# A decoder layer on one core: heads' outputs copied by ScalarE and scaled in SBUF, router constants on ScalarE, other spacing of the compression, the modulation and the first routing

## The chip, the cores and the metric

The kernel runs as one program on one core of a Trainium2 chip. The metric is the time of one execution in microseconds on the device. Before is given as the median of three runs. Five engines work side by side, each through its own queue in the order of the program: TensorE (PE, matrix products; PEld is its loading of weights), VectorE (DVE), ScalarE (ACT), GpSimd (POOL) and SyncE (SP), which issues most transfers.

## What is computed

One decoder layer over 1024 tokens of width 1024, with random weights in float32. Two groups of channels read the same modulated and normalised input: an attention with three branches (compressed blocks, blocks chosen by score, a window), gated and added up, and a short gated convolution. Both go through a norm of 64 channels each and an output projection; a mixture of 64 experts follows.

```
sh1, sc1, g1, sh2, sc2, g2 = split(silu(c) @ w_ada + b_ada)        # six rows of 1024
h = rms_norm(x, norm1_w) * (1 + sc1) + sh1
q, kvs, gate_logits, b_gate, c_gate, u = split(h @ w_in)
k_c = rms_norm(compress(kv[:, :, 0], cmp_pos_k, cmp_k_w1, cmp_k_w2), k_norm_w[0])
v_c = compress(kv[:, :, 1], cmp_pos_v, cmp_v_w1, cmp_v_w2)   # silu(blocks @ w1) @ w2
o_attn = nsa_attention(q, gates, k_c, v_c, k_s, v_s, k_w, v_w, rel_bias)
         # three branches for each head: gates[..., i] * softmax(...) @ v, added up
y_conv = b_gate * short_conv(c_gate * u, conv_w)
mix = rms_norm over each 64 channels of concat(o_attn, y_conv)
x = x + g1 * (mix @ w_out)
h2 = rms_norm(x, norm2_w) * (1 + sc2) + sh2
x = x + g2 * hier_moe(h2, w_group, b_group, w_expert, b_expert, w1, w3, w2)
         # top 1 of 8 groups, top 2 of its 8 experts, 64 experts in all
```

## The kernel before

The kernel is one long program for the five engines. Its stages in the order of time are: a head (the first modulation row by matmuls, the norm and the transposes of the input), the projection, the attention, the rest of the output projection with the routing of the second half of the tokens, and the experts, whose weights are streamed through a ring of buffers while TensorE multiplies.

The projection is cut into jobs of 128 columns. `job(idx, ...)` runs 48 matmuls of 128 by 512 (lines 367 to 369: three for each of 8 k-steps and each of two halves of the tokens), into the PSUM tags "pp" and "st". A k-step ends with `yield`. What a job's result needs afterwards (the copy, the norm's root, transposes) is a generator in the list `posts`; `advance()` moves every such generator by one step, once in the middle of each half of a job and once at its end. `cmp_post(kvi)` is such a generator. It makes the compressed keys (kvi 0) or values (kvi 1): a shifted copy S of the projection, a bias added into Z (line 579), a product with the weights w1 in four pieces (line 590, into "acc"), the silu through e into hid (lines 596 to 599), a product with w2 (line 605 for keys, line 628 for values), and for the keys a norm of 64 columns, jk (line 613), and a transpose (line 616). `value_post` copies the values and transposes them (line 678).

Beside this stands a second generator, `mod_steps`: the five chunks of the relative bias table (`rel_steps`, lines 167 to 170: matmul, two copies by VectorE, a DMA to memory from POOL, the copy of the next chunk waiting for it), reads back and twelve exchange matmuls (line 193), and then the sums of the remaining two thirds of the modulation (`ada_sums`, lines 295 and 297: for each of 8 pieces of 128 rows of the weight, one VectorE instruction on 128 by 1024; 16 instructions for each of two rows of the modulation), the matmuls that add up the partitions (line 306), and `ada_done` with its transposes (line 272). Each load of weights for it is issued two pieces ahead. `first_job(steps)` moves `mod_steps` by one at some k-steps of a job, and what is left at the end is issued behind the gate job.

The PSUM tags "mx", "pp", "st" and "acc" have two buffers of 128 by 512 each; `ps(tag)` takes the next one, and an instruction that writes it waits until the last reader of its content two turns earlier is done. "mx" is used by the relative table, the compression, the modulation and the transposes of values; "acc" by the compression's product with w1, by the norms of the projections and by the outputs of heads.

The attention has 16 units (a head and a half of the queries). For each tile of scores, ScalarE takes two exponentials, P and PH, VectorE or POOL their difference PL, and TensorE multiplies PH and PL with the values into an accumulator of "acc" (lines 948 to 951). When a branch of a unit is complete, `take` scales it by gate over sum and adds it to oN. `merge` norms two heads, and transposes them (line 974). The second half of the attention also carries, as filler, the preparation of the output projection (`out_prepare`, with the router's constants, lines 1101 and 1108), its matmuls and `route(0)`, the routing of the first half of the tokens.

## Time and profile before

| | before |
|---|---|
| median of three runs | 1701.32 us |
| the runs, lowest and highest | 1697.93 and 1703.72 us |
| profiled execution | 1703.64 us |
| its span, first to last instruction | 1701.9 us |
| granted clock of TensorE, mean over the span | 0.967 |
| busy TensorE | 1537.3 us (90%) |
| busy VectorE | 711.5 us (42%) |
| busy ScalarE | 512.3 us (30%) |
| busy GpSimd | 356.8 us (21%) |

All durations and positions in the rows below are of this one profiled execution, in us from the start of its span. The shares are means over the whole span; the projection, the attention and the experts each have another mix. "Idle before, and what ended it" says which instruction released a waiting one.

### The profile page before, as it was taken

How to read it: one execution, taken by the hardware profiler on the slowest of the kernel's cores; microseconds unless marked ns; L12 is line 12 of the kernel's file. 1: busy time of each engine (PE TensorE's matmuls, PEld its weight loads, DVE VectorE, ACT ScalarE, POOL GpSimd, SP SyncE). 2: the span in 40 equal slices, each digit the busy share in tenths (PEclk: the TensorE clock that was granted, in tenths of full speed). 3: DMA queues.
4: the chain of work that ended last, by engine and by line, in shares of the span. 5: the costliest groups of instructions: out<-in, count | busy, mean ns of one | idle time of the engine just before them, and what ended most of it. 6: DMA issues, size and time to landing. Idle time of an engine off the chain costs nothing. (4 is left out here: it accounts for less than half of the span.)

```text
span 1701.9 us, 24631 instructions
## 1 busy us (share of the span) xinstructions
PE 1537.3 (90%) x9870; PEld 733.9 (43%) x9870; DVE 711.5 (42%) x1678; ACT 512.3 (30%) x992; POOL 356.8 (21%) x355
## 2 busy tenths in 40 slices
PE   5978988999889998969999998999999999899995
PEld 3434454555456664533443334333333333343431
DVE  3737675565798666581323123214113112131211
ACT  4654655565566664120201011101002011020100
POOL 4233453344475545010000000000000000000000
PEclk8899989999999999979999999999999999999998
DMA  9338541110241115669999999999999999999992
GB/s 352 102 114 261 155 110 44 36 39 17 64 158 46 40 33 188 246 257 399 427 425 427 427 424 428 426 426 427 427 427 427 427 426 426 426 426 429 426 428 112
DMA packets 84627, 480.82 MB, mean 283 GB/s; under 512 B 12551, under 2 KB 46552, under 8 KB 58652
## 3 DMA queue, kind: packets, MB, share of 16 engines
q1 hardware_dynamic: 76620, 461.16, 67.3%
q0 software_dynamic: 7744, 18.03, 2.9%
q8 instruction: 79, 1.29, 0.3%
q14 instruction: 40, 0.33, 0.1%
q10 hardware_dynamic: 144, 0.00, 0.0%
HBM read 473.20 MB, written 14.35 MB: 286 GB/s over the span
## 5 line engine op out<-in xcount | busy, mean ns | idle before, releaser
L1573 PE MATMUL ps<-wr,xs 128*64 128x512 f32 x2048 | 453.4, 597 | 1.8 <-DVE xs L1563 1.0
L1590 PE MATMUL ps<-wr,hT 128*64 128x512 f32 x1024 | 258.0, 608 | 44.3 <-DMA wr<-in_w_dram 42.8
L1573 PEld LDWEIGHTS ps<-wr,xs 128*64 128x64 f32 x2048 | 158.3, 138 | 289.7 <-issue 248.8
L1560 ACT ACTIVATE xs<-ps,sh2p,a2p 128x128 f32<-128x128 f32 x128 | 55.1, 455 | 565.7 <-DVE xs L1563 563.2
L1485 DVE TENSOR_TENSOR hid<-ps,hid 128x512 f32<-128x512 f32 x32 | 22.1, 691 | 417.3 <-PE ps L1573 417.3
L1627 POOL DMA_INDIRECT out_dram<-xg,toki x16 | 15.9, 997 | 793.9 <-DVE xg L1626 793.2
L1590 PEld LDWEIGHTS ps<-wr,hT 128*64 128x64 f32 x1024 | 79.2, 140 | 215.4 <-issue 148.5
L877 POOL TENSOR_TENSOR PL<-P,PH 128x384 f16<-128x384 f32 (+3 forms) x138 | 131.2, 956 | 172.9 <-ACT PH L873 85.7
L1593 DVE TENSOR_TENSOR y<-ps,lt 128x512 f32<-128x512 f32 x64 | 44.3, 692 | 250.3 <-PE ps L1590 250.3
L871 ACT ACTIVATE P<-st 128x512 f32<-128x512 f32 (+3 forms) x208 | 98.3, 472 | 110.8 <-PE st L929 88.4
L1622 PE MATMUL sum<-y,CT 128*128 128x512 f32 x256 | 115.3, 593 | 0.0
L367 PE MATMUL pp<-hi,wh 128*128 128x512 f16 x272 | 105.8, 391 | 3.5 <-ACT hi L435 3.5
L369 PE MATMUL pp<-hi,wl 128*128 128x512 f16 x272 | 106.1, 390 | 0.0
L368 PE MATMUL pp<-lo,wh 128*128 128x512 f16 x272 | 105.8, 389 | 0.0
L873 ACT ACTIVATE PH<-st 128x512 f16<-128x512 f32 (+3 forms) x208 | 98.0, 471 | 0.3
L1484 ACT ACTIVATE hid<-ps 128x512 f32<-128x512 f32 x32 | 19.1, 597 | 197.2 <-PE ps L1573 197.2
L1622 PEld LDWEIGHTS sum<-y,CT 128*128 128x128 f32 x256 | 46.1, 190 | 46.8 <-issue 46.0
L1563 DVE TENSOR_SCALAR xs<-ps,a2p,sh2p 128x128 f32<-128x128 f32 x128 | 49.5, 407 | 39.5 <-ACT xs L1560 27.7
L948 PE MATMUL acc<-VH,PH 128*128 128x65 f16 x528 | 59.6, 196 | 5.2 <-DVE ot L895 5.2
L1555 PE MATMUL ps<-Sm,xl 128*128 128x128 f16 x512 | 61.6, 220 | 2.5 <-DVE xl L1522 2.5
L1555 PE MATMUL ps<-Sm,xh 128*128 128x128 f16 x512 | 61.7, 220 | 1.6 <-ACT xh L1521 1.6
L919 PE MATMUL st<-QA,KA 128*128 128x512 f16 (+1 forms) x192 | 60.7, 316 | 1.7 <-ACT PH L873 1.5
(448 smaller groups left out, 2531.5 us busy)
## 6 DMA issues: line engine op xcount, KB each, us to landing
wr<-in_w_dram SPq DMA_DIRECT2D x189, 2048.0 KB
ada<-in_w_ada_dram SPq DMA_DIRECT2D x32, 512.0 KB
raw<-in_w_in_dram SPq DMA_DIRECT2D x22, 512.0 KB
ada<-in_w_ada_dram SPq DMA_DIRECT2D x8, 1024.0 KB
xt<-in_x_dram SPq DMA_DIRECT2D x8, 512.0 KB
x<-in_w_out_dram SPq DMA_DIRECT2D x8, 512.0 KB
wr<-in_w_dram SPq DMA_DIRECT2D x3, 1024.0 KB
w1t<-in_cmp_k_w_dram POOLq DMA_DIRECT2D x4, 512.0 KB, 4.8
```

The costliest lines, as they stand in the source:

```text
L367: PE.matmul(p, wh[:, k, :], hi[:, k, m], start=(k == 0), stop=False)
L368: PE.matmul(p, wh[:, k, :], lo[:, k, m], start=False, stop=False)
L369: job_pe[0] = PE.matmul(p, wl[:, k, :], hi[:, k, m], start=False, stop=(k == KT - 1)).ins
L871: ACT.activation(P[:, c], p[:, c], AF.Exp)
L873: ACT.activation(PH[:, c], p[:, c], AF.Exp)
L877: eng.tensor_sub(PL[:, c], P[:, c], PH[:, c])
L919: PE.matmul(p[:, c], KA[g][:, j, b, :], tq[:, c], start=True, stop=False)
L948: PE.matmul(o, PH[:, w_], vh, start=(first and q == q0), stop=False, skip_group_check=True)
L1555: pe(PE.matmul(q[:, k * 128:(k + 1) * 128], part[:, a, h, k, :], Sm[:, a, sl], start=(a == 0 and part is xh), stop=(a == 1 and part is xl)))
L1573: pe(PE.matmul(hp_[nm][64 * u:64 * u + 64, :], xs[:, k, 64 * u:64 * u + 64], wring[nm, 2 * P + u, k], start=(k == 0), stop=(k == KT - 1)))
L1590: pe(PE.matmul(q[64 * u:64 * u + 64, :], hT[:, f, 64 * u:64 * u + 64], wring["w2", 2 * P + u, f][:, n * 512:(n + 1) * 512], start=(f == 0) ...
L1622: pe(PE.matmul(sums[a][n], CT[:, a, :], y[:, n * 512:(n + 1) * 512], start=(p == 0), stop=(p == 3)))
```

## The change

A modulation step is taken after every second k-step instead of every third. In `cmp_post`, three steps lie between hid and its product and, for the keys, three between jk and its transpose, instead of two and one. The transposes of the values and of the modulation write "acc" instead of "mx". In `take`, ScalarE copies the 260 columns of the accumulator into SBUF first, VectorE works from the copy, and the tile ot is no more. The router's eight broadcast columns shb and the eight scalings of WR are done by ScalarE. The last merged pair's scaling is done by VectorE instead of POOL. `route(0)` has eight more steps.

```
@@ -267,7 +267,7 @@
         yield
         POOL.dma_start(modD[s].rearrange("h (c j) -> c h j", c=4), modrow[s][0:128:32, :].rearrange("c (h j) -> c h j", h=2))
         yield
-        pt = ps()
+        pt = ps("acc")
         for t in range(4):
             PE.transpose(pt[:, t * 128:(t + 1) * 128], modrow[s][:, t * 128:(t + 1) * 128], identf)
         V.tensor_copy(modc[:, s * 16:(s + 1) * 16].rearrange("p (h c t) -> p h c t", h=2, c=4),
@@ -597,8 +597,8 @@
                 V.tensor_scalar(e, e, 1.0, None, op0=ALU.add)
                 V.reciprocal(e, e)
                 V.tensor_mul(hid[:, t, :], ph[t], e)
-            yield
-            yield
+            for _ in range(3):
+                yield
             if kvi == 0:
                 pk = ps()
                 for t in range(2):
@@ -611,7 +611,8 @@
                 V.tensor_scalar(sk[:, 0:1], sk[:, 0:1], 1.0 / HD, EPS, op0=ALU.mult, op1=ALU.add)
                 POOL.tensor_tensor(sk[:, 1:2], sk[:, 0:1], mhalf[:, 0:1], op=ALU.pow)
                 V.scalar_tensor_tensor(jk, pks, sk[:, 1:2], knc, op0=ALU.mult, op1=ALU.mult)
-                yield
+                for _ in range(3):
+                    yield
                 pt = ps()
                 PE.transpose(pt[0:64, 0:128], jk, identf)
                 for g in range(2):
@@ -673,7 +674,7 @@
             ACT.activation(vt, p, AF.Copy, scale=1.0 / WS)
             yield
             yield
-            pt = ps()
+            pt = ps("acc")
             for j in range(4):
                 PE.transpose(pt[:, j * 128:(j + 1) * 128], vt[:, j * 128:(j + 1) * 128], identf)
             src = pt.rearrange("p (j g d) -> p j g d", j=4, g=2)
@@ -718,7 +719,7 @@
 
     def first_job(steps):
         for n_, _ in enumerate(steps):
-            if n_ % 3 == 2:
+            if n_ % 2:
                 with tc.issue_after(job_pe[0]):
                     next(mod_steps, None)
 
@@ -879,7 +880,8 @@
 
     def take(u, acc, n, gi):
         half, h = units[u]
-        av = acc[:, 0:260].rearrange("p (i c) -> p i c", i=4)
+        av = aw.tile([128, 4, 65], F32, name="av")
+        ACT.activation(av, acc[:, 0:260].rearrange("p (i c) -> p i c", i=4), AF.Copy)
         r = aw.tile([128, 4], F32, name="rr")
         V.scalar_tensor_tensor(r, av[:, :, 64], 1e-27, gates[:, half * 4:half * 4 + 4, h * 3 + gi],
                                op0=ALU.max, op1=ALU.mult)
@@ -891,9 +893,8 @@
         if n == 0:
             V.tensor_tensor(dst, av[:, :, 0:64], rb, op=ALU.mult)
         else:
-            ot = aw.tile([128, 4, 64], F32, name="ot")
-            V.tensor_tensor(ot, av[:, :, 0:64], rb, op=ALU.mult)
-            POOL.tensor_tensor(dst, dst, ot, op=ALU.add)
+            V.tensor_tensor(av[:, :, 0:64], av[:, :, 0:64], rb, op=ALU.mult)
+            POOL.tensor_tensor(dst, dst, av[:, :, 0:64], op=ALU.add)
 
     def slots_of(u):
         half = units[u][0]
@@ -965,7 +966,7 @@
         V.tensor_reduce(so, sq8, axis=AX.X, op=ALU.add)
         V.tensor_scalar(so, so, 1.0 / HD, EPS, op0=ALU.mult, op1=ALU.add)
         POOL.tensor_tensor(so, so, mhalf, op=ALU.pow)
-        POOL.tensor_tensor(sq8, o8, so[:, :, None].to_broadcast([128, 8, 64]), op=ALU.mult)
+        (V if pr == 7 else POOL).tensor_tensor(sq8, o8, so[:, :, None].to_broadcast([128, 8, 64]), op=ALU.mult)
         for _ in range(MERGE_LAG):
             yield
         with tc.issue_after(last_pe[0]):
@@ -1098,14 +1099,14 @@
         PE.matmul(pb[:, 0:72], ones[0:1, :], rb, start=True, stop=False)
         for k in range(KT):
             shb = rt.tile([128, 128], F32, name="shb")
-            V.tensor_copy(shb, SH2[:, k:k + 1].to_broadcast([128, 128]))
+            ACT.activation(shb, SH2[:, k:k + 1].to_broadcast([128, 128]), AF.Copy)
             PE.matmul(pb[:, 0:72], shb, WR[:, k, :], start=False, stop=(k == KT - 1))
         R["io"] = rt.tile([128, GCAP], BF, name="io", bufs=1)
         POOL.iota(R["io"], pattern=[[1, GCAP]], base=0, channel_multiplier=0, allow_small_or_imprecise_dtypes=True)
         R["rbias"] = rt.tile([128, 72], F32, name="rbias", bufs=1)
         V.tensor_copy(R["rbias"], pb[:, 0:72])
         for k in range(KT):
-            V.tensor_scalar(WR[:, k, :], WR[:, k, :], a2[:, k:k + 1], None, op0=ALU.mult)
+            ACT.activation(WR[:, k, :], WR[:, k, :], AF.Identity, scale=a2[:, k:k + 1])
         yield
 
     def out_part(t, ks):
@@ -1222,6 +1223,9 @@
         G = tile_(8, "G")
         V.tensor_tensor(G, row(io64[:, 0:8]), wide(gid, 8), op=ALU.is_equal)
         V.tensor_copy(GA[:, ts, 0:8], G)
+        if hb == 0:
+            yield
+            yield
         pg = ranks(ps(tag), 0, 8)
         payA = rt.tile([128, 4, 2], F32, name="payA", bufs=1)
         payA3 = rt.tile([128, 4, 3, 2], BF, name="payA3", bufs=1)
@@ -1237,6 +1241,9 @@
             oh = rt.tile([128, GCAP], BF, name="oh0", bufs=4)
             oh_ = V.tensor_scalar(oh, R["io"], t0[:, i, :], None, op0=ALU.is_equal)
             ohs.append(oh)
+        if hb == 0:
+            yield
+            yield
         table(tabA, payA3, 2, tabA if hb else crow[:, :, 6:8].to_broadcast([128, 2, 2]))
         if hb:
             V.tensor_copy(toki0, tabA[:, :, 0])
@@ -1263,6 +1270,9 @@
         V.tensor_tensor(es, eo[:, :, 0, :], eo[:, :, 1, :], op=ALU.add)
         V.tensor_tensor(GA[:, ts, 8:72].rearrange("p t (g e) -> p t g e", g=8), G[:, :, :, None].to_broadcast([128, 4, 8, 8]),
                         es[:, :, None, :].to_broadcast([128, 4, 8, 8]), op=ALU.mult)
+        if hb == 0:
+            yield
+            yield
         pe_ = ranks(ps(tag), 8, 64)
         if hb == 0:
             R["GS"] = rt.tile([128, 72], BF, name="GS", bufs=1)
@@ -1296,6 +1306,9 @@
 
         V.tensor_copy(payB3[:, :, 0, 0:2], sl1)
         V.tensor_sub(payB3[:, :, 1, 0:2], sl1, payB3[:, :, 0, 0:2])
+        if hb == 0:
+            yield
+            yield
         table(tab0, payB3, 4, tab0 if hb else crow[:, :, 1:5].to_broadcast([128, 2, 4]))
         V.tensor_scalar(ok, r01, float(CAP), None, op0=ALU.is_lt)
 
```

On TensorE in the projection, around line 616 (which is line 617 after the change), the transpose of the compressed keys; wh, wl, hi and lo are the operands of projection matmuls, nf those of the exchange matmuls. Before:

```order
L369 LDWEIGHTS wl
L369 MATMUL st<-hi,wl 128x512
L616 MATMUL mx<-identf,jk 64x128
L367 LDWEIGHTS wh
L367 MATMUL st<-hi,wh 128x512
L368 LDWEIGHTS wh
L368 MATMUL st<-lo,wh 128x512
L193 LDWEIGHTS exch
L193 MATMUL mx<-nf,exch 128x512
```

After:

```order
L369 LDWEIGHTS wl
L369 MATMUL pp<-hi,wl 128x512
L617 MATMUL mx<-identf,jk 64x128
L679 MATMUL acc<-identf,vt 128x128 x4
L367 LDWEIGHTS wh
L367 MATMUL st<-hi,wh 128x512
L368 LDWEIGHTS wh
L368 MATMUL st<-lo,wh 128x512
L369 LDWEIGHTS wl
```

Before, the transpose stood 12 projection matmuls behind the product of line 605 and two ahead of an exchange matmul; now it stands 36 behind, and the transposes of values follow it. The exchange matmuls are issued earlier.

On TensorE, around line 306, the matmuls that add up the modulation's sums (the tile acc on the right is a sum on VectorE, acc on the left a PSUM buffer, Z the compression's operand). Before, the first of the two rows:

```order
L369 LDWEIGHTS wl
L369 MATMUL pp<-hi,wl 128x512
L306 MATMUL acc<-acc,ones 32x256 x8
L367 LDWEIGHTS wh
L367 MATMUL pp<-hi,wh 128x512
L368 LDWEIGHTS wh
L368 MATMUL pp<-lo,wh 128x512
L369 LDWEIGHTS wl
```

After, the first of the two rows:

```order
L369 MATMUL pp<-hi,wl 128x512
L306 MATMUL acc<-acc,ones 32x256 x4
L590 MATMUL acc<-Z,w1t 128x128 x8
L367 LDWEIGHTS wh
L367 MATMUL st<-hi,wh 128x512
L368 LDWEIGHTS wh
L368 MATMUL st<-lo,wh 128x512
L369 LDWEIGHTS wl
L369 MATMUL st<-hi,wl 128x512
L367 LDWEIGHTS wh
L367 MATMUL st<-hi,wh 128x512
L306 MATMUL acc<-acc,ones 32x256 x4
```

Before, the eight matmuls stood together behind 402 projection matmuls; now the first four stand behind 264 and the other four behind 268, between pieces of the values' product with w1. The second row's matmuls stood behind the gate job and now stand behind 384.

On ScalarE in the attention, around the first copies of heads' outputs (P and PH are the exponentials of scores st, av the new copy, wh and y belong to the filler). Before:

```order
L871 ACTIVATE P<-st 128x384
L873 ACTIVATE PH<-st 128x384
L871 ACTIVATE P<-st 128x256
L873 ACTIVATE PH<-st 128x256
L342 ACTIVATE wh<-raw 128x1024
L751 ACTIVATE y<-z,vcols 128x512
L871 ACTIVATE P<-st 128x128
```

After:

```order
L874 ACTIVATE PH<-st 128x384
L884 ACTIVATE av<-acc 128x260
L872 ACTIVATE P<-st 128x256
L874 ACTIVATE PH<-st 128x256
L884 ACTIVATE av<-acc 128x260
L342 ACTIVATE wh<-raw 128x1024
L752 ACTIVATE y<-z,vcols 128x512
L872 ACTIVATE P<-st 128x128
```

The copy stands between the two exponentials of one tile of scores and those of the next, and nothing on ScalarE was removed for it.

## Rows read from the trace of the kernel before

**Rows 1.** Busy time of each engine by stretch of the span: from to (us), length, then busy us of each engine with its instructions in brackets, TensorE's granted clock (1.00 is full), the mean busy share of the 16 DMA engines, GB/s. The projection jobs, the attention, the expert layer.
```profile
47.00:223.00 176.00, 156.04 (x913) 79.37 (x913) 115.79 (x185) 98.32 (x155) 62.96 (x48) 0.93 0.51 158
225.00:672.00 447.00, 407.19 (x3913) 245.98 (x3905) 302.02 (x867) 263.90 (x564) 225.34 (x224) 0.98 0.20 62
757.00:1669.00 912.00, 864.62 (x4407) 351.15 (x4408) 217.00 (x388) 113.09 (x215) 30.15 (x29) 0.99 1.00 425
```

**Rows 2.** The same view, four stretches of 20 us within the projection.
```profile
100.00:120.00 20.00, 12.07 (x47) 4.72 (x45) 6.10 (x17) 12.62 (x23) 8.47 (x9) 0.83 0.29 83
...
140.00:160.00 20.00, 14.12 (x75) 7.52 (x75) 19.25 (x24) 8.38 (x14) 7.55 (x4) 0.95 0.86 266
...
200.00:220.00 20.00, 18.86 (x168) 9.60 (x167) 17.78 (x27) 12.20 (x19) 10.25 (x7) 0.93 0.71 225
220.00:240.00 20.00, 14.91 (x170) 8.67 (x167) 17.32 (x21) 10.98 (x20) 11.02 (x8) 0.76 0.49 133
```

**Rows 3.** What TensorE waited for between 80 and 240 us: engine, tile, line, what it waited for, us in total, times, longest.
```profile
PE mx L616 <- DVE jk L613: 5.1, 1, 5.1
PE mx L678 <- DVE VCH L630: 3.1, 1, 3.1
PE mx L628 <- DVE hid L599: 2.8, 1, 2.8
PE mx L193 <- DVE pks L609: 1.9, 1, 1.9
PE acc L306 <- DVE acc L295: 4.4, 1, 4.4
PE mx L272 <- DVE parts L824: 2.2, 1, 2.2
```

**Rows 4.** The same view as the first table of stretches, the stretches behind five of these waits.
```profile
110.00:114.00 4.00, 3.91 (x11) 1.51 (x12) 3.29 (x11) 2.47 (x5) 0.03 (x1) 0.52 0.02 4
160.00:165.00 5.00, 5.00 (x13) 1.81 (x12) 4.54 (x6) 2.87 (x6) 3.13 (x2) 0.50 0.96 238
234.00:240.00 6.00, 5.82 (x31) 3.15 (x32) 3.35 (x12) 1.94 (x5) 2.14 (x3) 0.50 0.02 2
296.00:300.00 4.00, 4.00 (x15) 1.84 (x13) 1.40 (x4) 1.92 (x3) 2.34 (x4) 0.50 0.00 0
```

**Rows 5.** Groups of instructions between 47 and 240 us: line, engine, operation, out<-in, shapes, count | busy us, mean ns of one | idle before, and what ended it.
```profile
L295 DVE SCALAR_TENSOR_TENSOR acc<-ada,ccol,acc 128x1024 f32<-128x1024 f32 x28 | 44.5, 1589 | 6.1 <-DMA ada<-in_w_ada_dram 6.0
L579 DVE TENSOR_TENSOR Z<-S,pos 128x1008 f32<-128x1008 f32 x4 | 7.5, 1918 | 0.0
L168 DVE CAST oz<-mx 8x512 f16<-8x512 f32 x4 | 2.7, 676 | 7.2 <-DMA relHD<-oz 7.1
```

**Rows 6.** Two projection matmuls on TensorE at the full granted clock, six starts apart: start us, duration us.
```profile
167.02 0.38 PE L369 MATMUL st<-hi,wl 128*128 128x512 f16 x1
...
168.31 0.38 PE L369 MATMUL st<-hi,wl 128*128 128x512 f16 x1
```

**Rows 7.** Lines 295 (the sums of the modulation rows on VectorE), 306 (the matmuls that add them up) and 711 (the last matmul of a step of the gate job): durations in ns (min/median/max), first and last start in us.
```profile
L295 DVE SCALAR_TENSOR_TENSOR acc<-ada,ccol,acc x28: 1187/1285/3154, 134.2 to 231.9; 128x1024 f32<-128x1024 f32 x28
L306 PE MATMUL acc<-acc,ones x32: 379/391/636, 188.1 to 234.6; 128*32 128x256 f32 x32
L711 PE MATMUL st<-wh,lo x64: 172/181/181, 217.6 to 223.0; 128*128 128x24 f16 x64
```

**Rows 8.** Groups of instructions between 240 and 675 us, columns as those of the groups above.
```profile
L895 DVE TENSOR_TENSOR ot<-acc,rr 128x256 f32<-128x256 f32 x32 | 13.5, 422 | 0.7
L884 DVE SCALAR_TENSOR_TENSOR rr<-acc,gates 128x4 f32<-128x4 f32 x48 | 7.4, 154 | 24.2 <-PE acc L951 24.2
L871 ACT ACTIVATE P<-st 128x256 f32<-128x256 f32 x39 | 14.9, 381 | 22.5 <-PE st L929 20.1 <-PE mx L846 1.2 <-POOL PL L877 0.9
L877 DVE TENSOR_TENSOR PL<-P,PH 128x256 f16<-128x256 f32 x16 | 9.5, 596 | 1.8 <-ACT PH L873 1.5
L1101 DVE COPY shb<-modc 128x128 f32<-128x128 f32 x8 | 2.7, 373 | 0.0
L1108 DVE TENSOR_SCALAR WR<-WR,a 128x72 f32<-128x72 f32 x8 | 2.6, 360 | 0.1
L968 POOL TENSOR_TENSOR osq<-oN,so 128x512 f32<-128x512 f32 x8 | 8.3, 1041 | 0.5
```

**Rows 9.** What TensorE waited for in the whole run, the row of the attention's takes.
```profile
PE acc L948 <- DVE ot L895: 5.2, 3, 3.0
```

**Rows 10.** Stretches in the second half of the attention, at its end, and ahead of the expert layer, columns as in the tables of stretches above.
```profile
452.00:530.00 78.00, 62.52 (x705) 40.36 (x702) 73.47 (x174) 53.20 (x114) 57.54 (x54) 0.96 0.36 116
640.00:675.00 35.00, 26.82 (x316) 17.77 (x313) 24.55 (x111) 16.15 (x39) 20.33 (x23) 0.98 0.51 169
740.00:745.00 5.00, 5.00 (x32) 2.02 (x28) 0.03 (x1) 0.46 (x1) 0.00 (x0) 0.81 0.09 32
```

**Rows 11.** What TensorE waited for between 640 and 680 us, the three longest.
```profile
PE mx L974 <- POOL osq L968: 3.3, 1, 3.3
PE acc L951 <- DVE PL L877: 2.0, 2, 1.6
PE pp L1190 <- DVE GA L1224: 1.1, 1, 1.1
```

**Rows 12.** What the queue that loads weights waited for.
```profile
SPq L1027 <- PE ps L1573: 603.4, 65, 32.0
```

More of the change, by code (lines that the diff above doesn't have):

```diff
@@ L269, in ada_done @@
         yield
-        pt = ps()
+        pt = ps("acc")
         for t in range(4):
@@ L599, in post @@
                 V.tensor_mul(hid[:, t, :], ph[t], e)
-            yield
-            yield
+            for _ in range(3):
+                yield
             if kvi == 0:
@@ L613, in post @@
                 V.scalar_tensor_tensor(jk, pks, sk[:, 1:2], knc, op0=ALU.mult, op1=ALU.mult)
-                yield
+                for _ in range(3):
+                    yield
                 pt = ps()
@@ L675, in post @@
             yield
-            pt = ps()
+            pt = ps("acc")
             for j in range(4):
@@ L720, in first_job @@
         for n_, _ in enumerate(steps):
-            if n_ % 3 == 2:
+            if n_ % 2:
                 with tc.issue_after(job_pe[0]):
@@ L881, in take @@
         half, h = units[u]
-        av = acc[:, 0:260].rearrange("p (i c) -> p i c", i=4)
+        av = aw.tile([128, 4, 65], F32, name="av")
+        ACT.activation(av, acc[:, 0:260].rearrange("p (i c) -> p i c", i=4), AF.Copy)
         r = aw.tile([128, 4], F32, name="rr")
@@ L893, in take @@
         else:
-            ot = aw.tile([128, 4, 64], F32, name="ot")
-            V.tensor_tensor(ot, av[:, :, 0:64], rb, op=ALU.mult)
-            POOL.tensor_tensor(dst, dst, ot, op=ALU.add)
+            V.tensor_tensor(av[:, :, 0:64], av[:, :, 0:64], rb, op=ALU.mult)
+            POOL.tensor_tensor(dst, dst, av[:, :, 0:64], op=ALU.add)
     def slots_of(u):
@@ L967, in merge @@
         POOL.tensor_tensor(so, so, mhalf, op=ALU.pow)
-        POOL.tensor_tensor(sq8, o8, so[:, :, None].to_broadcast([128, 8, 64]), op=ALU.mult)
+        (V if pr == 7 else POOL).tensor_tensor(sq8, o8, so[:, :, None].to_broadcast([128, 8, 64]), op=ALU.mult)
         for _ in range(MERGE_LAG):
@@ L1100, in out_prepare @@
             shb = rt.tile([128, 128], F32, name="shb")
-            V.tensor_copy(shb, SH2[:, k:k + 1].to_broadcast([128, 128]))
+            ACT.activation(shb, SH2[:, k:k + 1].to_broadcast([128, 128]), AF.Copy)
             PE.matmul(pb[:, 0:72], shb, WR[:, k, :], start=False, stop=(k == KT - 1))
@@ L1107, in out_prepare @@
         for k in range(KT):
-            V.tensor_scalar(WR[:, k, :], WR[:, k, :], a2[:, k:k + 1], None, op0=ALU.mult)
+            ACT.activation(WR[:, k, :], WR[:, k, :], AF.Identity, scale=a2[:, k:k + 1])
         yield
@@ L1224, in route @@
         V.tensor_copy(GA[:, ts, 0:8], G)
+        if hb == 0:
+            yield
+            yield
         pg = ranks(ps(tag), 0, 8)
@@ L1239, in route @@
             ohs.append(oh)
+        if hb == 0:
+            yield
+            yield
         table(tabA, payA3, 2, tabA if hb else crow[:, :, 6:8].to_broadcast([128, 2, 2]))
@@ L1265, in route @@
                         es[:, :, None, :].to_broadcast([128, 4, 8, 8]), op=ALU.mult)
+        if hb == 0:
+            yield
+            yield
         pe_ = ranks(ps(tag), 8, 64)
@@ L1298, in route @@
         V.tensor_sub(payB3[:, :, 1, 0:2], sl1, payB3[:, :, 0, 0:2])
+        if hb == 0:
+            yield
+            yield
         table(tab0, payB3, 4, tab0 if hb else crow[:, :, 1:5].to_broadcast([128, 2, 4]))
```

## The prediction

> **What bounds the kernel now.** I read the busy times by stretch first. In the projection TensorE works 156 of 176 us, in the attention 407 of 447 [rows 1]: it is the engine that nearly always has work, so the change can only pay by what TensorE stands still or runs at half clock. The expert layer behind it is another thing: there the DMA share is 1.00 for 912 us [rows 1], and the weights set its pace. When it starts, the DMA share is 0.09 with TensorE at work [rows 10], and the weight queue's largest wait of the run is for TensorE to use up what is loaded, 603 us [rows 12]. The buffers are full, so what is won or lost ahead of it reaches the end one to one. The change touches nothing in it.
>
> Next, the waits of TensorE by stretch. In the projection six of them, 19.5 us together (5.1 + 3.1 + 2.8 + 1.9 + 4.4 + 2.2), hang on values that the compression, the modulation or their shared PSUM tag "mx" deliver late [rows 3]. Behind the longest the granted clock is 0.52 for 4 us, 0.50 for 5 us and 0.50 for 6 us [rows 4], the lower of TensorE's two levels (1.2 GHz); work that ran at half speed there cost 1.9 + 2.5 + 3.0 = 7.4 us. So 26.9 us lie open. The 4.4 us stand behind all projection work, when only the sums of the last modulation rows are missing.
>
> **The change, part by part.**
>
> *Modulation steps after every second k-step, compression spread out.* Removed: the whole 26.9 us could go. Line 616's product is wanted 36 job matmuls behind line 605 instead of 12; one takes 0.215 us (168.31 minus 167.02 over six, [rows 6]), so its cover grows from 2.6 to 7.7 us against a chain that was 5.1 late. Line 628 gets 48 behind the last line 590 instead of 24. The transposes of v and of the modulation leave "mx", where 3.1 and 2.2 us were waited for a buffer. Both groups of line 306 now stand before the gate job; before, they ran from 188.1 to 234.6 us while the gate job's matmuls ended at 223.0 [rows 7].
>
> Added: three things. First, the five chunks of the relative table come within 41 job matmuls from count 66 on, before within 42 from 81 on. Each chunk's copy on VectorE waited for the DMA of the chunk before, 7.2 us over the four large ones [rows 5], and three of those DMAs now stand behind a weight load on POOL's queue. What stands behind a waiting copy on VectorE is the compression's own input, Z, which TensorE wants next: I take 4 us, between 2 (hidden as before) and 6 (most of the old wait anew on TensorE). Second, the sums. Thirty-two of them, 28 at a mean of 1589 ns [rows 5], took 97.7 us of the span (134.2 to 231.9, [rows 7]). At a step per six job matmuls they would lie in 32 x 6 x 0.215 = 41 us, and the 28 alone want 44.5 [rows 5]. VectorE was busy 19.25 of 20 us where they lay thick, and 17.8 and 17.3 in the last two stretches [rows 2]. So VectorE becomes the bound from the nearest-moved sum to the last: TensorE will wait anew at the second line 590 for Z (1.9 us an instruction [rows 5], four of them with sums between), at the second group of line 306, and again at line 628. I take 13 us of such waits, from a floor of 3 (44.5 us of sums in 41 us) to a ceiling of 25 (all the old waits and a quarter more). Third, the half clock behind them, 4 us, between 0 and the old 7.4. "acc", with two buffers, now also carries v's transposes; I price that within the 13. Sum: 26.9 - 21 = 6 us won, between 22 won and 12 lost.
>
> *Heads' outputs through ScalarE.* TensorE's next value matmuls waited 5.2 us for line 895 to free the accumulator, in three places [rows 9], and behind one of them the clock was 0.50 for 4 us, 2.0 us lost [rows 4]: 7.2 us. Now a copy frees it. A copy of 260 columns should take what a 256-column exponential does, 381 ns, against 154 + 422 ns and a reciprocal on VectorE [rows 8], and ScalarE, busy 264 of 447 us [rows 1], is freer than VectorE, busy 302. The copies are 48 x 0.381 = 18.3 us more for ScalarE. What hides them is its own idle time: 20.1 us before the 256-column exponentials alone were spent waiting for scores [rows 8]. I take half of the 7.2, 3.5 won, between 7.2 won and 3 lost (one copy in six in front of an exponential that TensorE waits for).
>
> Line 877's product on VectorE with both operands in SBUF takes 596 ns for 256 columns, line 895's from PSUM 422 [rows 8]. The scaling now has both operands in SBUF. The Trainium skill's page "SBUF — State Buffer", section "Who interferes with whom", says that a VectorE instruction with two SBUF inputs and a GpSimd one that reads SBUF lock each other out; the gap of 174 ns is in line with it. By that, each of the 48 scalings is 0.17 us longer, some 8 us of VectorE in the attention, 1.5 of them in the 78 us where it has no room [rows 10]; this part would be 2 won instead of 3.5.
>
> *Router constants to ScalarE.* Sixteen instructions leave VectorE, 2.7 + 2.6 us [rows 8], in a stretch of 78 us where it is busy 73.5 and TensorE only 62.5 [rows 10]. ScalarE is busy 53.2 there and takes them. TensorE waits there for POOL's products too, so less than half comes through: 2 won, between 4 and 0.
>
> *First routing over eight more steps, last scaling on VectorE.* Between 640 and 675 us TensorE is idle 8.2 us [rows 10], 3.3 of them for the last merged head, 2.0 for a product and 1.1 for the routing [rows 11]. The last table moves behind the last attention matmul, and 22 instead of 17 output matmuls then stand ahead of the merged head's transposes: 5 x 0.215 = 1.1 us more cover. On POOL the scaling took 1041 ns [rows 8]; on VectorE twice 422 is the nearest, 0.2 us less. So 1.3 of the 3.3 go, the routing's 1.1 goes, and a third of the product's 2.0: 3 won. If the table's own chain is then waited for at the end, it can lose 2; if all three waits go, it wins 6.
>
> Sum: 6 + 3.5 + 2 + 3 = 14.5 us won. The profiled execution took 1703.6, so 1689.1 there; it lay 2.3 above the median of the runs, so **1687**.
>
> **The rivals.**
>
> *The sums make VectorE the bound, and the gain stays there.* For it: 44.5 us of sums against 41 us of slots, and a longest sum of 3154 ns against a median of 1285 [rows 7]: they are dearer when something else runs. If their mean goes from 1589 to about 2000 ns, 28 x 0.41 = 11.5 us of the 14.5 are gone: 1698, which is no change. Against it: the sums are only waited for at line 306, twice.
>
> *The other side: the same sums dearer still.* The point is a mean of about 2.3 us, 28 x 0.7 = 20 us more on an engine that already bounds the stretch: 5.5 slower than before, 1707. The stretches with most sums also had the DMA share at 0.86 [rows 2]. Against it: no stretch so far shows a mean that high.
>
> *ScalarE takes over VectorE's wait, also slower.* Line 884 waited 24.2 us for the accumulator [rows 8]. The copy inherits that wait, and exponentials stand behind it. If they all came late by as much, the attention would be 24.2 longer: 1711, and from 20 us on slower than before by a measurable amount. Against it: the next exponentials want scores that TensorE computes only behind the value matmuls the copy waits for. The Trainium skill, "ScalarE: Activation LUTs", "Rules for kernel authors", advises VectorE for plain multiplications and additions; by that rule the copies and constants are misplaced, and this case is where it would be right. The rows' reason against it is that VectorE has no room.
>
> *More than I take.* If the spreading works as written and the new waits are at their floor (2 + 3 + 0), 22 are won in the projection and 30 in all: 1671. If half of that comes, 1679.
>
> *Nothing reaches the end.* If the weights set the end whatever comes before, 1701. The DMA share of 0.09 at the start of the layer speaks against it.
>
> **How the numbers follow.** Forecast 0.50 (its own range 1680 to 1695); more than I take 0.13; sums as bound, no change, 0.17; sums dearer, slower, 0.09; ScalarE 0.06; nothing reaches the end 0.05. A measurement can tell about 0.3%, 5.1 us, from no change. Faster 0.63, same 0.22, slower 0.15. The range leaves out the lower half of "more" and most of the slower cases: 1673 to 1706.
>
> **What the profile will show.** Right: no wait of line 616 for jk, none over 1 us of line 948 for the accumulator, both groups of line 306 ended before the gate job, the gate job ended at 214 to 223 us, the attention started within 3 us of it, sums at a mean below 1.9 us. ScalarE's copies at about 0.39 us. Wrong: line 306 or 590 waiting over 8 us; VectorE busy over 95% from 110 to 180 us with the gate job later than 226; exponentials waiting for the accumulator with TensorE idle behind them; a wait for payB or osq over 4 us at the end.

## The result: slower by 1.5 per cent, most of it in the attention

| | before | after |
|---|---|---|
| median | 1702.28 us (4 runs) | 1726.76 us (4 runs) |
| ratio to before | 1 | 1.0147, 95% interval 1.0131 to 1.0163 |
| profiled execution's span | 1701.9 us | 1723.9 us |
| granted clock, mean | 0.967 | 0.962 |

The change made the kernel some 25 us slower; 14.5 us faster had been forecast. The expert layer is as long as before. The kernel after falls behind as it goes: three marks show where. First two lines of the kernel before, the reading of a head's output (first and last start at the end of each line) and the first matmul of the experts; the columns are durations in ns (min/median/max), then first and last start in us:

```profile
L884 DVE SCALAR_TENSOR_TENSOR rr<-acc,gates x48: 124/156/164, 250.2 to 666.2; 128x4 f32<-128x4 f32 x48
L1573 PE MATMUL ps<-wr,xs x2048: 592/592/1114, 739.1 to 1659.9; 128*64 128x512 f32 x187
```

The lines of after that answer to them, and to lines 306 and 711 of [rows 7] (lines behind 600 have moved by 1 to 13):

```profile
L306 PE MATMUL acc<-acc,ones x32: 379/379/403, 146.2 to 188.3; 128*32 128x256 f32 x32
L712 PE MATMUL st<-wh,lo x64: 172/173/173, 222.5 to 227.5; 128*128 128x24 f16 x64
L884 ACT ACTIVATE av<-acc x48: 372/393/432, 253.2 to 682.0; 128x260 f32<-128x260 f32 x48
L1586 PE MATMUL ps<-wr,xs x2048: 592/592/1116, 760.7 to 1682.1; 128*64 128x512 f32 x187
```

The gate job ends 4.5 us later (227.5 against 223.0), though the modulation's sums are complete 46 us earlier (188.3 against 234.6). The first head's output is taken 3.0 us later, the last 15.8 later, the experts start 21.6 later and their last matmul starts 22.2 later. So some 3 to 5 us are lost ahead of the attention, 13 in it, and 6 between it and the experts. The first of the three is hardly more than the spread of single executions: in the nine profiles whose projection is that of before, the gate job ends between 221.0 and 225.3 us and the first rr starts between 245.3 and 253.2 (254.4 in after). The second and third have to be read together; e4 below shows why. That what is lost ahead of the experts reaches the end one to one was right.

TensorE's waits of after between 60 and 240 us, as [rows 3]:

```profile
PE acc L590 <- issue: 8.2, 1, 8.2
PE mx L193 <- DMA nf<-relHD: 6.5, 2, 5.1
PE st L920 <- ACT gates L717: 4.4, 1, 4.4
PE acc L644 <- DVE t L650: 3.6, 1, 3.6
PE mx L617 <- DVE jk L613: 0.7, 1, 0.7
```

The old waits have mostly gone (line 617 was 5.1 as line 616, 1.7 of the 2.8 of line 628 are left at line 629, and lines 306, 678 and 272 are off the list), and new ones as long have come. The one at line 590 is put down to "issue". VectorE's and TensorE's instructions around its end (start us, duration us) show what it is:

```profile
135.36 1.83 DVE L579 TENSOR_TENSOR Z<-S,pos 128x1008 f32<-128x1008 f32 x1
137.12 1.26 DVE L295 SCALAR_TENSOR_TENSOR acc<-ada,ccol,acc 128x1024 f32<-128x1024 f32 x1
138.31 1.83 DVE L579 TENSOR_TENSOR Z<-S,pos 128x1008 f32<-128x1008 f32 x1
```

```profile
140.24 2.05 PE L590 MATMUL acc<-Z,w1t 128*128 128x128 f32 x8 [8.18 <-issue]
```

The second half of Z ends at 140.14, with a sum between the two halves, and TensorE starts at 140.24: the wait is for Z. TensorE's waits of after in the attention, 225 to 690 us:

```profile
PE acc L952 <- POOL PL L878: 9.7, 12, 3.2
PE acc L952 <- DVE PL L878: 6.6, 5, 1.8
PE mx L837 <- DVE parts L825: 6.4, 9, 2.2
PE mx L852 <- DVE parts L825: 4.8, 3, 3.4
...
PE acc L949 <- ACT av L884: 2.0, 1, 2.0
```

The same view of before, where these lines stand one lower:

```profile
PE acc L951 <- DVE PL L877: 5.6, 7, 1.6
PE acc L951 <- POOL PL L877: 5.5, 8, 1.4
...
PE mx L851 <- DVE parts L824: 1.9, 3, 1.4
...
PE mx L836 <- DVE parts L824: 1.0, 2, 0.8
```

The wait for the accumulator, 5.2 us in [rows 9], is down to 2.0, as meant. But other waits have grown. At parts, VectorE reads a buffer of "mx" that TensorE wants to fill again; the two waits for it went from 2.9 to 11.2 us. Those for the products PL of both engines went from 11.1 to 16.3. The groups of after that answer to [rows 8] say why (as there; the last number is idle time before it):

```profile
L886 DVE SCALAR_TENSOR_TENSOR rr<-av,gates 128x4 f32<-128x4 f32 x48 | 20.6, 429 | 4.5 <-ACT av L884 4.1
L884 ACT ACTIVATE av<-acc 128x260 f32<-128x260 f32 x48 | 18.9, 394 | 2.4 <-PE acc L952 2.2
L896 DVE TENSOR_TENSOR av<-av,rr 128x256 f32<-128x256 f32 x32 | 17.5, 546 | 0.5
L894 DVE TENSOR_TENSOR oN<-av,rr 128x256 f32<-128x256 f32 x16 | 7.2, 453 | 0.4
```

The smallest instruction of a take, 128 by 4, went from 154 to 429 ns in the mean, and the scaling from 422 to 546. Nothing in it but the place of its operands is different. One of them on VectorE, and what GpSimd did at that time (start us, duration us):

```profile
435.38 0.76 DVE L886 SCALAR_TENSOR_TENSOR rr<-av,gates 128x4 f32<-128x4 f32 x1
```

```profile
435.20 0.92 POOL L878 TENSOR_TENSOR PL<-P,PH 128x384 f16<-128x384 f32 x1 [5.08 <-PE pp L368]
```

It ends at 436.14, 0.02 us after GpSimd's subtraction at 436.12. Read this way through the 48 takes of after: in 23 no GpSimd operation lies over rr, and it takes 157 ns; in 25 one does, and it takes 680 in the mean. Of these, 21 end within 0.05 us of a GpSimd operation; the other four take 157 to 161, as GpSimd's operation was over within that time or began after them. In the kernel before, 28 of the 48 lie under a GpSimd operation, too, and take 154 ns all the same: there the first operand comes from PSUM.

### The profile page after: what moved, and what is told of

It reads as the page before. It is cut to its first block, busy times and chain, and to the rows that moved or that the text cites. A ratio compares the mean times of both kernels' runs of the same rounds, so it can differ in the third digit from the quotient of the medians.

```text
span 1723.9 us, 24684 instructions
## 1 busy us (share of the span) xinstructions
PE 1544.3 (90%) x9870; PEld 738.1 (43%) x9870; DVE 722.8 (42%) x1663; ACT 528.4 (31%) x1056; POOL 349.5 (20%) x354
## 5 line engine op out<-in xcount | busy, mean ns | idle before, releaser
L1603 PEld LDWEIGHTS ps<-wr,hT 128*64 128x64 f32 x1024 | 83.2, 140 | 212.3 <-issue 144.9
L878 DVE TENSOR_TENSOR PL<-P,PH 128x512 f16<-128x512 f32 (+3 forms) x70 | 45.3, 647 | 44.6 <-ACT PH L874 33.7
```

What stands on the lines that cost most here:

```text
L878: eng.tensor_sub(PL[:, c], P[:, c], PH[:, c])
L1603: pe(PE.matmul(q[64 * u:64 * u + 64, :], hT[:, f, 64 * u:64 * u + 64], wring["w2", 2 * P + u, f][:, n * 512:(n + 1) * 512], start=(f == 0) ...
```

## The experiments

All ratios are to the kernel before, measured beside it on the same chip.

**The change in four parts.** e1 is the takes alone:

```
-        av = acc[:, 0:260].rearrange("p (i c) -> p i c", i=4)
+        av = aw.tile([128, 4, 65], F32, name="av")
+        ACT.activation(av, acc[:, 0:260].rearrange("p (i c) -> p i c", i=4), AF.Copy)
...
-            V.tensor_tensor(ot, av[:, :, 0:64], rb, op=ALU.mult)
-            POOL.tensor_tensor(dst, dst, ot, op=ALU.add)
+            V.tensor_tensor(av[:, :, 0:64], av[:, :, 0:64], rb, op=ALU.mult)
+            POOL.tensor_tensor(dst, dst, av[:, :, 0:64], op=ALU.add)
```

> The kernel before with the heads' outputs alone changed (copy of 260 columns by ScalarE, VectorE scaling from SBUF). Theory A (the takes carry the loss: the reading of the gates' ratio rr went from 154 to 430 ns a piece, 48 of them, when both its inputs were in SBUF, and the copies stand in ScalarE's queue ahead of exponentials): 12 to 18 us slower than before. Theory B (the shift of the projection's and the routing's filler carries it, the takes are harmless): within 5 us of before. The prediction's term: 3.5 us faster.

Measured: 1722.82 us against 1703.11, ratio 1.0116 (1.0099 to 1.0134), 19.7 us slower. Theory A.

e2 is the projection's four edits:

```
-        pt = ps()
+        pt = ps("acc")                    # modulation's and values' transposes
...
-            yield
-            yield
+            for _ in range(3):
+                yield                     # before hid's product; the same before jk's transpose
...
-            if n_ % 3 == 2:
+            if n_ % 2:
```

> The kernel before with the projection's four edits alone (modulation step every second k-step, three steps for the compression, transposes of values and modulation in the tag acc). Theory A: 3 to 5 us slower, as the gate job ends 4.5 us later in the profile of after and the first take stands 2.9 us later. Theory B: 10 us slower or more, since the filler of the attention is shifted as well. The prediction's term: 6 us faster.

Measured: 1705.97 against 1703.11, ratio 1.0019 (1.0005 to 1.0033), 3.2 us slower. Its two longest waits between 60 and 240 us are those of after:

```profile
PE acc L590 <- issue: 7.8, 1, 7.8
PE mx L193 <- DMA nf<-relHD: 5.9, 2, 4.9
```

e3 is the router's constants:

```
-            V.tensor_copy(shb, SH2[:, k:k + 1].to_broadcast([128, 128]))
+            ACT.activation(shb, SH2[:, k:k + 1].to_broadcast([128, 128]), AF.Copy)
...
-            V.tensor_scalar(WR[:, k, :], WR[:, k, :], a2[:, k:k + 1], None, op0=ALU.mult)
+            ACT.activation(WR[:, k, :], WR[:, k, :], AF.Identity, scale=a2[:, k:k + 1])
```

> The kernel before with the router's constants alone moved to ScalarE. Theory A: within 3 us of before. Theory B: 3 to 8 us slower, because the lost stretch between 505 and 540 us is where these sixteen instructions lie, and they stand ahead of exponentials. The prediction's term: 2 us faster.

Measured: 1702.61 against 1703.11, ratio 1.0001 (0.9987 to 1.0015): no difference that can be told.

e4 is the first routing with its eight steps and the last scaling:

```
-        POOL.tensor_tensor(sq8, o8, so[:, :, None].to_broadcast([128, 8, 64]), op=ALU.mult)
+        (V if pr == 7 else POOL).tensor_tensor(sq8, o8, so[:, :, None].to_broadcast([128, 8, 64]), op=ALU.mult)
...
+        if hb == 0:
+            yield
+            yield
```

> The kernel before with the first routing's eight more steps and the last pair's scaling on VectorE alone. Theory A: 2 to 6 us slower, since in after the time from the last take to the expert layer grew by 5 us. Theory B: within 3 us of before, as that growth comes from output matmuls that the slower attention left over. The prediction's term: 3 us faster.

Measured: 1704.32 against 1703.11, ratio 1.0006 (0.9993 to 1.0018): no difference that can be told. The four ratios add to 1.42 per cent, the whole change is 1.47: the takes alone are four fifths of it. The traces also show where the 6 us that after loses behind the attention come from. First e4, then e1, with rr and the first matmul of the experts:

```profile
L884 DVE SCALAR_TENSOR_TENSOR rr<-acc,gates x48: 128/156/164, 250.4 to 662.1; 128x4 f32<-128x4 f32 x48
L1585 PE MATMUL ps<-wr,xs x2048: 592/592/1112, 739.6 to 1660.5; 128*64 128x512 f32 x187
```

```profile
L885 DVE SCALAR_TENSOR_TENSOR rr<-av,gates x48: 131/167/1161, 251.4 to 685.4; 128x4 f32<-128x4 f32 x48
L1573 PE MATMUL ps<-wr,xs x2048: 592/592/1116, 757.8 to 1678.7; 128*64 128x512 f32 x187
```

From the first rr to the last it is 415.9 us in before, 411.8 in e4 and 434.0 in e1; from the last rr to the experts 72.9, 77.5 and 72.4. In all thirteen profiles without the routing's edit this second stretch is 71.1 to 73.0 us, in the three with it 77.5 to 79.4. So the first routing moves 4 to 5 us from the attention to behind it, at no cost in sum, and the takes lose all of their 18 us in the attention. The change has both (428.3 and 78.1). The reason that theory B gives, work left over by a slower attention, falls, as e4's attention is not slower.

**What the takes cost.** e5 puts the copy in front without using it:

```
         av = acc[:, 0:260].rearrange("p (i c) -> p i c", i=4)
+        ac = aw.tile([128, 4, 64], F32, name="ot")
+        ACT.activation(ac, av[:, :, 0:64], AF.Copy)
```

> The kernel before, with a copy of the 256 output columns by ScalarE that nobody uses; VectorE still reads the accumulator in PSUM, so the accumulator is free only after both. Left out of the change: all reading from SBUF. Theory A1 (VectorE and GpSimd hold each other up when VectorE reads two operands in SBUF): within 4 us of before, rr at about 155 ns. Theory A2 (the copies stand in ScalarE's queue ahead of exponentials that TensorE wants): 12 to 20 us slower, as the takes alone were.

Measured: 1711.00 against 1699.60, ratio 1.0065 (1.0043 to 1.0088), 11 us slower, between the two theories. Its rr takes 155 ns as before, but stands behind the copy:

```profile
L886 DVE SCALAR_TENSOR_TENSOR rr<-acc,gates 128x4 f32<-128x4 f32 x48 | 7.5, 155 | 7.0 <-ACT ot L884 6.5
```

That was not planned: VectorE waits in this program for ScalarE's copy (none of the 48 starts before it has ended), though both only read the accumulator. And ScalarE's copies waited 6.9 us for accumulators themselves. So the run holds the copy in series, a longer hold of the accumulator and ScalarE's waiting, and not ScalarE's time alone. In its profile the stretch from the first rr to the last is 420.6 us, against 413.9 to 416.9 in the eight profiles with the takes and the routing of before, so the 11 us may be on the high side.

e6 is the takes of the change with one operand moved back:

```
-        V.scalar_tensor_tensor(r, av[:, :, 64], 1e-27, gates[...], op0=ALU.max, op1=ALU.mult)
+        V.scalar_tensor_tensor(r, acc[:, 0:260].rearrange("p (i c) -> p i c", i=4)[:, :, 64], 1e-27, gates[...],
+                               op0=ALU.max, op1=ALU.mult)
```

> The takes of the change, but rr, the ratio of gate and sum, read from the accumulator in PSUM and not from the copy; the scaling still reads the copy. Theory A1, with the lock's cost in rr (13 us more busy time of VectorE over 48 pieces): rr back at about 155 ns, 4 to 9 us slower than before instead of 19.7. Theory A2: still 15 to 20 us slower.

Measured: 1716.73 against 1699.60, ratio 1.0094 (1.0070 to 1.0119), 16 us slower: rr is back at 154 ns, but the time came back by some 4 us only, and the intervals of e1 and e6 overlap. The wait moved on. The scaling, now first in line with both operands in SBUF, took 652 ns instead of e1's 538 (line 895), and TensorE stood 4.2 us for the accumulator that rr still holds, behind the copy as in e5:

```profile
PE acc L948 <- DVE rr L885: 4.2, 4, 2.9
```

e9 asks whether it is ScalarE's time at all:

```
+        ac = aw.tile([128, 4, 64], F32, name="ot")
+        ACT.activation(ac.rearrange("p i c -> p (i c)")[:, 0:192], gates.rearrange("p t c -> p (t c)"), AF.Copy)
```

> The kernel before, with 48 copies by ScalarE that nobody uses, at the places of the heads' outputs, but of 192 columns of the gates in SBUF: ScalarE's time is taken (about 0.34 us each against 0.39), it waits for no accumulator and holds none. Theory L (the 11 us of the copy-only run are ScalarE's time, exponentials that come later): 7 to 11 us slower. Theory H (they are the waiting for the accumulator and its later release): within 3 us of before.

Measured: 1702.41 against 1702.88, ratio 1.0000 (0.9985 to 1.0015). These copies are 17.5 us of ScalarE, and no cost can be told, to 2.6 us either way:

```profile
L884 ACT ACTIVATE ot<-gates 128x192 f32<-128x192 f32 x48 | 17.5, 365 | 9.6 <-POOL oN L898 5.5 <-DVE gates L717 3.8
```

So ScalarE has that much time to give, as theory H says. But these copies do not stand where e5's do in ScalarE's queue: the first two lie behind none and two of the attention's exponentials P and PH, those of e5 behind 14 and 22. What is left for the 11 us of e5 is the copy's place in the chain (TensorE, ScalarE, VectorE, GpSimd, each in order), the accumulator held meanwhile, and exponentials that come late behind a copy at that place. No run tells these three apart.

e12 and e13 take ScalarE out and differ in where rr and the scaling read. e12 makes the copy on VectorE and works from it; e13 makes a copy there too (256 columns instead of 260), does not use it and works from PSUM. So in e12 the accumulator is free behind the copy, in e13 only behind the scaling:

```
+        V.tensor_copy(av, acc[:, 0:260].rearrange("p (i c) -> p i c", i=4))     # e12, the rest as in the change
...
+        ac = aw.tile([128, 4, 64], F32, name="ot")
+        V.tensor_copy(ac, av[:, :, 0:64])                                        # e13, the rest as before
```

> The takes of the change, but the copy into SBUF is made by VectorE, so no engine stands between TensorE and VectorE; the scaling then has both operands in SBUF. Compared with e13 only. Theory A1 (two SBUF operands on VectorE against GpSimd): rr near 400 ns and the scaling near 530 ns, 6 to 14 us slower than e13. Theory A3 (what costs is only that an engine more stands in the chain of a take and its queues): within 3 us of e13, or faster, since the accumulator is free earlier.

> The kernel before with a copy by VectorE that nobody uses, at the same place; the scaling reads PSUM as before. VectorE has about 20 us more work in the attention, rr stays at 155 ns, the accumulator is free 0.4 us later than before. Theory A1: 3 to 10 us slower than before. Theory A3: as e12 within 3 us.

Measured: e12 1718.54 against 1699.54, ratio 1.0113 (1.0089 to 1.0136); e13 1709.95, ratio 1.0046 (1.0028 to 1.0064). The medians are 8.6 us apart, the ratios 0.67 per cent or 11 us (6 to 16 by the two intervals), and from the first rr to the last it is 432.9 against 425.8 us. Groups of e12:

```profile
L885 DVE SCALAR_TENSOR_TENSOR rr<-av,gates 128x4 f32<-128x4 f32 x48 | 21.4, 445 | 0.3
L895 DVE TENSOR_TENSOR av<-av,rr 128x256 f32<-128x256 f32 x32 | 17.9, 561 | 0.5
L893 DVE TENSOR_TENSOR oN<-av,rr 128x256 f32<-128x256 f32 x16 | 9.3, 579 | 0.3
```

and of e13:

```profile
L886 DVE SCALAR_TENSOR_TENSOR rr<-acc,gates 128x4 f32<-128x4 f32 x48 | 7.3, 151 | 0.0
L897 DVE TENSOR_TENSOR ot<-acc,rr 128x256 f32<-128x256 f32 x32 | 13.4, 420 | 1.1 <-POOL oN L898 0.2
L894 DVE TENSOR_TENSOR oN<-acc,rr 128x256 f32<-128x256 f32 x16 | 6.7, 420 | 0.3
```

The same work is 21.4 + 17.9 + 9.3 = 48.6 us of VectorE from SBUF and 27.4 from PSUM. TensorE's two waits for parts, between 225 and 690 us, first in e12, then in e13:

```profile
PE mx L836 <- DVE parts L824: 6.3, 8, 2.3
...
PE mx L851 <- DVE parts L824: 3.4, 2, 2.2
```

```profile
PE mx L851 <- DVE parts L824: 1.8, 2, 1.4
PE mx L836 <- DVE parts L824: 1.4, 3, 0.8
```

They are 9.7 and 3.2 us, and they sort the other runs as well: 11.0 in e1, where rr reads SBUF, but 4.7 in e6, 3.5 in e5 and 2.9 in before, where it reads PSUM. This shows that two operands in SBUF beside a busy GpSimd cost 7 to 11 us here by themselves, with the accumulator even freed earlier, and that much of it (9.7 less 3.2 us) reaches TensorE through readings of "mx" that come later on VectorE. The other 9 to 13 of the 19.7 us of e1 are not taken apart further.

e7 is the changed kernel with the takes of before:

> The changed kernel with the takes of before. If the terms add up: 24.5 minus 19.7, so 2 to 7 us slower than before. If the takes cost so much only with the shifted filler: anything else; faster than before by 3 us or more if the other parts help once the attention isn't held up.

Its edit is the diff of the change without its two hunks at lines 879 and 891. Measured: 1708.81 against 1699.60, ratio 1.0048 (1.0028 to 1.0068): 8 us slower, a little above the 2 to 7 expected; the lower end of the interval, 4.8, lies just above the sum of e2 to e4, 4.4.

**The projection.** e8 is the rate of the modulation alone:

```
-            if n_ % 3 == 2:
+            if n_ % 2:
```

> The kernel before with the modulation step at every second k-step alone. My theory (in the profile of after TensorE stood 8.2 us at line 590 behind the wait of VectorE and 6.5 us at line 193 for the table's read back): 2 to 6 us slower, gate job ending 3 us or more later. The rival (the extra turns of acc and the compression's three steps carry the 3.2 us): within 1.5 us or faster.

Measured: 1704.34 against 1699.60, ratio 1.0030 (1.0019 to 1.0042), 5 us slower. The gate job ends at 228.9 us. TensorE's longest wait between 60 and 240 us is the one for the reading back, while that of line 590 for Z is 0.5:

```profile
PE mx L193 <- DMA nf<-relHD: 6.5, 2, 5.0
```

e10 is the other three edits of the projection without this one:

> The kernel before with the compression's three steps and the transposes of values and modulation in the tag acc, modulation steps at every third k-step as before. Theory M (the faster modulation steps are what costs in the projection, 5 us alone, and the rest won 2 back): 2 to 6 us faster. Rival (the two accumulator buffers take back what the compression wins): within 2 us of before.

Its edit is that of e2 without its last two lines. Measured: 1699.54 against 1702.88, ratio 0.9986 (0.9969 to 1.0003): 2.4 us faster by the ratio, an interval that just holds no change. It leans to theory M and doesn't prove it.

e11 keeps all four and puts five empty modulation steps more ahead of the exchange matmuls of line 193:

```
-        for _ in range(4):
+        for _ in range(9):
             yield
         for n_, (i, dst, off) in enumerate(jobs_):
```

> The four edits of the projection as in e2, with nine empty modulation steps instead of four between the reading back of the relative table and its first exchange matmul. In e2 TensorE stood 5.9 us at line 193 for that reading back. Theory M1 (that wait is the loss of the projection): 3 to 6 us faster than e2, so 0 to 3 us faster than before. Theory M2 (the sums ahead of Z on VectorE, 7.8 us at line 590, are the loss; the wait at line 193 only moves the same work): within 2 us of e2.

Measured: 1695.93 against 1702.88, ratio 0.9960 (0.9943 to 0.9977), 7 us faster than before and 10 faster than e2. Between 60 and 240 us TensorE waits:

```profile
PE acc L590 <- issue: 6.4, 1, 6.4
PE acc L306 <- DVE t L650: 4.4, 1, 4.4
PE st L920 <- ACT gates L717: 4.0, 1, 4.0
PE mx L193 <- ACT nh L194: 3.2, 3, 1.7
```

The wait for the reading back is gone, those of Z and of the gates are still there. So theory M2 is out, and M1 named a wait that went; that the edit gives 10 us (6 to 14 by the two intervals) and not the 5.9 it lasted is more than either theory said. The edit does more than part these matmuls from their input: the sums come out of the same generator and are put off too (line 295 runs from 119.9 to 197.3 us, in e2 from 114.4 to 187.1), and the waits of e2 at line 644 (4.2 and 1.9 us), 629 (1.8) and 617 (1.4) are off the list as well. How much of the 10 us is the reading back alone is open.

e14 adds e3's edit to e11:

> The projection's edits with nine empty steps, as in e11, and the router's constants on ScalarE, as in e3; takes and first routing as before. If the terms add up: 6 to 8 us faster than before, the same as e11 within 2 us, since the constants alone changed nothing.

Measured: 1692.16 against 1699.54, ratio 0.9946 (0.9928 to 0.9964), 9 us faster than the kernel before and by the ratios 34 faster than the change. It is the version that the runs point to. That the constants add something to e11 is not shown, as the two intervals overlap.

## Why the prediction was wrong, point by point

**What bounds the kernel.** Right: TensorE's idle time ahead of the experts decides, and the loss there (21.6 us) reached the end (22.2). The rival that nothing reaches the end is out.

**Heads' outputs, 3.5 us won: this step failed, by 23 us.** The rows for it were there. The prediction read line 877 against line 895 in [rows 8] and saw that two operands in SBUF cost more, and then charged it to the scaling alone, 0.17 us for each, 8 us in all, of which 1.5 would come through. Two things were wrong. The cost was charged by size, but it is a wait for GpSimd's running instruction, so that the first instruction of the take pays it however small it is: rr, 128 by 4, also has two operands in SBUF after the change (av and gates), and alone it went from 7.4 to 20.6 us. The profile of before had it already: of the 16 instructions of line 877 whose mean is 596 ns, the nine with no GpSimd operation over them take 421 ns, as line 895 does from PSUM, and the seven others 822. All in all VectorE had 20.6 + 17.5 + 7.2 = 45.3 us for what took 27.6 before (7.4 and 13.5 in [rows 8], and 6.7 for the first branch, as in e13), 17.7 more against 8. And 19 per cent of it was assumed to reach TensorE; e12 and e13 show 7 to 11 of 21 us. The Trainium skill's page cited there, "SBUF — State Buffer", says in its section "SBUF: two separate sides" that the one of the two that starts first keeps the other fully blocked for its whole instruction, and the trace agrees: 21 of the 25 pieces under a GpSimd operation end with it. The wait should have been the forecast's price instead of a sentence beside it.

The other part of the step was the chain. The copy was thought to replace 0.75 us of VectorE by 0.38 of ScalarE ahead of the accumulator's release. That came true (line 948 waits 2.0 us, not 5.2), and ScalarE had the time, as the idle rows had it (e9). But the scaling got an engine more ahead of it, and GpSimd's addition stands behind the scaling in GpSimd's own queue, ahead of the products TensorE wants: the wait for them went from 5.5 to 9.7 us. The prediction asked what the copy delays on ScalarE and not what it delays on VectorE and GpSimd. That this order is what made the wait grow is argued and not shown. e5 puts a price of 11 us (7 to 15) on the copy in front, but the accumulator is held longer in it than in the change, and exponentials can be late behind the copy; what the chain alone costs is open.

**The rival ScalarE** foresaw a slower kernel in the right part, for the wrong reason: ScalarE's copies waited 2.2 us for the accumulator, not 24.2, and TensorE's wait for an exponential at line 919 (now 920) went from 1.5 to 3.1 us. Exponentials that were late by way of the products PL are not told apart.

**The projection, 6 us won: 3.2 lost.** The old waits mostly went, as forecast. The new ones were put at 13 us, and the four longest of after are 8.2 + 6.5 + 4.4 + 3.6 = 22.7. The wait for Z was expected and is the largest; the 3.6 are for a buffer of "acc", which was priced within the 13. Two were missed. The exchange matmuls of line 193 moved ahead, from 100.4 us to 88.4, and what they read is read back from memory after the chunk chain: 5.1 us at one matmul. The chunk chain itself was priced, its consumer was not. e8 and e11 point to it as what decides, with the reservation above: with five steps more between, the four edits win 7 us. And behind the gate job, the attention's first matmul waits 4.4 us for the gates, where the matmuls of the last sums had stood and waited 4.4 before. The gates' exponential was late itself: in ScalarE's queue it stands behind line 341, which waited 4.0 us for a block of projection weights from memory:

```profile
231.78 1.06 ACT L341 ACTIVATE raw<-raw 128x1024 f32<-128x1024 f32 x1 [3.98 <-DMA raw<-in_w_in_dram]
...
234.03 0.33 ACT L717 ACTIVATE gates<-st 128x192 f32<-128x192 f32 x1
```

Two of the prediction's signs of being wrong came: line 590 waits over 8 us, and the gate job ends later than 226, though with VectorE busy 90 and not 95 per cent from 110 to 180 us (62.7 of 70). The rival of dearer sums fell: their mean is 1573 ns (1589 before, [rows 5]), though VectorE was busy 19.8 of 20 us between 120 and 140.

```profile
L295 DVE SCALAR_TENSOR_TENSOR acc<-ada,ccol,acc 128x1024 f32<-128x1024 f32 x28 | 44.0, 1573 | 4.6 <-DMA ada<-in_w_ada_dram 4.3
120.00:140.00 20.00, 11.30 (x51) 4.76 (x49) 19.77 (x24) 7.82 (x12) 5.75 (x4) 0.91 0.76 222
```

**Router's constants, 2 us won: none seen.** e3 shows no difference; its interval, from 2.2 us faster to 2.6 slower, just holds the forecast. VectorE was relieved in the stretch of 78 us [rows 10], but TensorE's wait for GpSimd's products at line 951 there is 5.1 us in before and 7.0 in e3.

**First routing, 3 us won: nothing, at most 3 lost.** e4 shows no difference, from 1.2 us faster to 3.1 slower. The wait for the last merged head is 3.3 us as before [rows 11]; only its name is VectorE now, which does the scaling:

```profile
PE mx L975 <- DVE osq L969: 3.3, 1, 3.3
```

The five more output matmuls ahead of it were not the cover they were counted as, and what left the attention came back behind it.

## What to carry to other kernels

Before a VectorE operation's input is moved from PSUM to SBUF, count its operands and look at what GpSimd does at that time: here an operation with two operands in SBUF waited for GpSimd's running instruction to end, and a tiny one waited as long as a large one. When an instruction is put on an engine with idle time, follow the chain behind it through every in-order queue, not only the queue that it joins. And when a producer chain is moved ahead, look at where its consumer then stands: here five empty steps ahead of the consumer, and of all that comes behind it in the same generator, turned 3 us lost into 7 won.

## What the runs showed of the hardware

A VectorE instruction of 128 by 4 took 154 ns with one operand in PSUM, whatever GpSimd did, and 157 ns with both in SBUF and GpSimd free, but 680 in the mean and up to 1161 with a GpSimd operation over it (after; in e12 up to 1922). In the attention of this kernel 17.5 us more of ScalarE, in copies that wait for nothing of TensorE's, cost nothing that can be told (e9), and 20.0 us more of VectorE, with the scaling and the accumulator's release 0.4 us later each time, 8 us (e13).
